# Hybrid Hyena and attention step: the weighted values of two query blocks in one PSUM bank of their own, and three banks for the seven-product pairs

## The chip, the cores and the metric

The kernel runs on one core of a Trainium2 chip. The metric is the device time of one execution in microseconds (us); lower is better. The core has a matrix engine (TensorE, "PE" in the profile; its weight loads are shown apart as "PEld"), a vector engine ("DVE"), a scalar engine ("ACT"), GpSimd ("POOL") and a queue that only issues transfers ("SP"). Products land in PSUM, which has eight banks of 128 partitions by 512 float32 values. Each engine works through its own instructions in the order in which they were put into its queue, and waits there for what an instruction needs.

## The reference, cut to what matters

One layer of a model with two parallel branches: a long convolution (Hyena) and attention. The change touches the attention branch. 512 latent queries attend to an 8 x 16 window of keys around them, plus 128 cached context keys, in one softmax; 128 prompt queries attend to the 128 prompt keys. There are 16 heads of 64 channels.

```python
s_win = einsum("brqhd,brkhd->bhrqk", qg, kg) * scale       # windowed keys, plus a learned bias
s_ctx = einsum("brqhd,bkhd->bhrqk", qg, ctx_k) * scale     # cached keys
p = softmax(concatenate([s_win, s_ctx], axis=-1), axis=-1)
o = einsum("bhrqk,brkhd->brqhd", p[..., :n_slab], vg) \
  + einsum("bhrqk,bkhd->brqhd", p[..., n_slab:], ctx_v)    # the weighted values
out = merge_branches(y_h, g_h, y_a, g_a, m, w_bh, w_ba, w_out)   # y_a * silu(g_a), projections, gates
x_new = layer_norm(ALPHA * x + gate * out, ln_g, ln_b)
```

## The kernel before, in words

The columns of every activation are the 640 tokens: 128 prompt tokens and 512 latent ones, the latter reordered into eight blocks of 64. Projections use each float32 operand as a high and a low part and add three products (high·high, high·low, low·high). A plain projection (line 177) fills two PSUM banks, one for each half of 320 columns.

Most projections of the attention stage are done two weight tiles at a time by `pair_tile` (lines 1167 to 1206): a 2 x 2 block product with seven products instead of eight. Each product is twelve matmuls of 128 x 320 into one of four PSUM tiles, x, y, v, z, in the order x, y, v, z, x, v, z; the last three add onto what is already there. Between the products the vector and scalar engines read the banks: after product 0 the scalar engine copies x to a tile `u` (line 1189); after product 1 the vector engine adds y to it (line 1191, "the u add"), which is the last read of y; after products 2, 3, 5 and 6 the vector engine adds v or z to that sum (line 1197); after product 4 the finished x is used directly. These four tiles come from `acc`, a pool of four banks that are handed out in turn; the other four banks, `aux`, serve all shorter uses.

There are 19 such pairs in the attention stage (queries and keys, attention gates, merge gates) and four more for `w_ba` afterwards. A generator `attend(j)` for each of the eight pairs of heads j is woven into them. It has *visits*, `tiled(i)` (lines 1084 to 1100), each for two query blocks of 128: the scores of the two blocks and two heads go into four `aux` banks; then come the weighted values of the two blocks of two visits earlier; then the softmax of the new scores. `turned(i)` transposes the probabilities of the last visit through `aux` banks and copies them to `pts` tiles. The weighted values of one block, `block_values` (lines 1071 to 1077), are three chunks of 128 keys times two heads: six float32 matmuls that each have 64 value channels as weights and move 128 query columns (line 1026). They are written to columns 384 to 511 of one of the score banks of the new visit, which the scores leave free. `gated` (lines 1062 to 1069) multiplies the result with the gate on the vector engine and sends it to DRAM (`ya_d`). An odd visit also has the prompt's weighted values.

Order: in the attention stage and in the stage after it TensorE runs in program order, as the weaving wrote it (`manual_schedule`). The vector, scalar and GpSimd instructions are ordered by a planner that simulates the program: of the instructions that are ready in its simulation it takes the one that stands first in the program. In the last stage (`out_tile`, line 1534) TensorE is left to the planner too.

After the attention stage, eight plain projections for `w_bh` (two banks each from `acc`) run, then the four `w_ba` pairs, then five output tiles, of which the first four take two `acc` banks each. Counted over the whole program, `acc` has been called 78 times when the attention stage starts.

Of the kernel before, what the change touches and what calls it, by code (L numbers as in the profile page):

```python
# [19 lines left out]
NT = 640  # L20
# [26 lines left out]
def tile_hyena_natten_step(ctx: ExitStack, tc: tile.TileContext, a, o):  # L47
# [59 lines left out]
    def split(dst_h, dst_l, src, eng=None):  # L107
        hi = nc.scalar.activation(dst_h, src, AF.Copy)  # L108
# [715 lines left out]
    def rows(h):  # L824
        return slice(64 * h, 64 * h + 64)
# [161 lines left out]
    def probs(j, b, s, tm):  # L987
# [15 lines left out]
        return res  # L1003

    CHUNKS = (
        ((2, 128), (1, 0), (None, 256)),
        ((2, 0), (3, 256), (None, 128)),
        ((3, 0), (4, 256), (None, 128)),
        ((4, 128), (1, 256), (None, 0)),
    )  # L1010

    def transposed(j, b, ps):
        res = []
        for h in range(2):
            pt = aux(f"pt{j}_{h}_{b}")
            parts = [ps[h][:, c : c + P] for _, c in CHUNKS[b]] + ([head[j]["pp"][:, h]] if b == 2 else [])
# [3 lines left out]
            ptS = at.tile([P, 384 if b % 2 else 512], F32, tag=f"pts{b % 2}", bufs=2, name=f"pts{j}_{h}_{b}")  # L1020
            nc.scalar.activation(ptS[:, :n], pt[:, :n], AF.Copy)
            res.append(ptS)
        return res

    def pvm(dst, lhs, rhs, start, stop):
        nc.tensor.matmul(dst, lhs, rhs, start=start, stop=stop, skip_group_check=True)  # L1026
# [33 lines left out]
        return out[f"v{j // 2}"][:, c : c + 64]  # L1060

    def gated(j, o_, *spans):
        yo = tp.tile([P, P], F32, tag="yo", bufs=3, name=f"yo{j}")
        c0 = 0
        for cols in spans:
            n = cols.stop - cols.start
            nc.vector.tensor_tensor(yo[:, c0 : c0 + n], out[f"sg{j}"][:, cols], o_[:, c0 : c0 + n], op=ALU.mult)
# [11 lines left out]
    def prompt_values(j, o_):  # L1079
        for h in range(2):  # L1080
            pvm(o_[rows(h)], val(j, 0, h), head[j]["t", 2][h][:, 384:], True, True)
        gated(j, o_, PS_)

    def tiled(i):
        ns = [n for n in (2 * i, 2 * i + 1) if n < 4 * NK]
        ss = {n: [aux(f"s{n}_{h}") for h in range(2)] for n in ns} or {0: [aux(f"ov{i}_{h}") for h in range(2)]}
        spare = [t[:, 384:] for n, pair in ss.items() if n % 4 or not ns for t in pair]
# [5 lines left out]
        j, b = divmod(2 * i - 4, 4)  # L1093
        if b == 2 and j >= 0:
            if not spare:
                spare.append(aux(f"op{j}")[:, 384:])
            prompt_values(j, spare.pop(0))
            del head[j]
# [26 lines left out]
    RING = ("wh", "wl", "wl", "wh", "wl")  # L1125

    ready, high, loads = {}, {}, {}

    def prepare(i0, i1, pin):
# [8 lines left out]
        s_cols = 512 if i0 >= T_BH else NT  # L1138

        def wsum(j, x, y, op, dst=None):  # L1140
            src[j] = dst if dst is not None else sp.tile([P, s_cols], F32, tag="s", bufs=3 if i0 >= T_BH else 2, name=f"s{j}_{i0}")[:, :512]
# [24 lines left out]

    def pair_tile(i0, i1, use, operand=operand):
        def halfrow(tag, bufs, name):
            return sp.tile([P, HALF if i0 >= T_BH else 384], F32, tag=tag, bufs=bufs, name=f"{name}{i0}")[:, :HALF]

        if i0 not in ready:
            prepare(i0, i1, False)
        wb, prep = ready.pop(i0)
        ps = {}
        for j in range(7):
            if j < 4:
                ps["xyvz"[j]] = acc(f"sp{i0}_{j}")[:, :HALF]
            dst, x = ps["xyvzxvz"[j]], operand(ORDER[j])
            for k in range(4):
                wh, wl = (wb[j][:, i, P * k : P * k + P] for i in range(2))  # L1180
                for i, (wk, xi) in enumerate(((wh, 0), (wh, 1), (wl, 0))):
                    nc.tensor.matmul(  # L1182
                        dst, wk, x(xi, k), start=j < 4 and k == 0 and i == 0, stop=k == 3 and i == 2, skip_group_check=True,
                    )
                if k == 1:
                    yield
            if j == 0:
                u = halfrow("u", 1, "u")
                nc.scalar.activation(u, dst, AF.Copy)
            elif j == 1:  # L1190
                nc.vector.tensor_tensor(u, dst, u, op=ALU.add)
            elif j == 4:
                use(0, 0, dst)
            else:
                if j != 3:
                    c = halfrow("c", 4, f"c{j}_")
                after = nc.vector.tensor_tensor(c, dst, c if j == 3 else u, op=ALU.add)  # L1197
# [25 lines left out]
    def mix(m):  # L1223
        t0, dst = (T_MH, mh_d) if m < 4 else (T_MA, ma_d)
        n0 = 2 * (m % 4)

        def use(i, hf, src):
            th = sp.tile([P, 384], F32, tag="c", bufs=4, name=f"th{m}")[:, :HALF] if hf == i == 0 else src
# [482 lines left out]
```

## Time and profile before

| what | value |
|---|---|
| time, median of 3 runs | 861.96 us (860.74 to 863.33) |
| profiled execution, span from first to last instruction | 859.1 us |
| time around the span, taken as median less span | 2.9 us |
| TensorE busy in the span | 849.4 us (99%) |
| VectorE busy | 678.7 us (79%) |
| ScalarE busy | 464.7 us (54%) |
| GpSimd busy | 131.4 us (15%) |
| mean granted TensorE clock | 0.998 |

The profile lists one execution. Only the span of that execution is in it; what lies around the span is taken as the difference to the median. A busy TensorE is not one at its best: matmuls overlap in a pipeline, and a group's mean is the duration of one from start to end, not the distance to the next. The distance between starts is what adds up; it is read from rows that give the start of a run of matmuls and their count.

### The profile page before, as it was taken

Reading aid. Unit: us, or ns where it says so; the run is one execution under the profiler, and the core shown is the slowest. Engines: PE = TensorE matmul, PEld = TensorE weight load, DVE = VectorE, ACT = ScalarE, POOL = GpSimd, SP = SyncE. Lnnn points to the kernel's source line nnn. Section 1 sums busy time; section 2 is a strip of 40 time slices with the busy share of each in tenths; the row PEclk is TensorE's granted clock in tenths of the full one; section 3 lists DMA queues with packets and bytes.
Section 4 is the critical chain, followed back from the end, with each engine's and each line's share of the span. In section 5 each row is a group of like instructions: output and inputs, shape, how many; then the busy total and the mean of one; then the engine's idle time right before and its main releaser. Section 6 shows DMA issues by size and latency. Waiting matters only on the chain.

```text
span 859.1 us, 16817 instructions
## 1 busy us (share of the span) xinstructions
PE 849.4 (99%) x6387; PEld 822.7 (96%) x6387; DVE 678.7 (79%) x1408; ACT 464.7 (54%) x996; POOL 131.4 (15%) x140
## 2 busy tenths in 40 slices
PE   9999999999999999999999999999999999999996
PEld 7999999999999999999999999999999999999885
DVE  6777695697759559789988897889888778799776
ACT  4675656545554643646665676666655654345310
POOL 0010010101001010105232225124222200000000
PEclk9999999999999999999999999999999999999999
DMA  9986575656657558774263535354354386445621
GB/s 352 359 256 144 109 149 126 153 122 144 127 134 150 126 146 187 168 251 148 85 195 90 192 95 189 106 177 149 105 173 118 111 266 202 173 131 140 246 107 54
DMA packets 56868, 138.64 MB, mean 161 GB/s; under 512 B 8495, under 2 KB 23859, under 8 KB 56788
## 3 DMA queue, kind: packets, MB, share of 16 engines
q1 hardware_dynamic: 45412, 111.69, 39.7%
q0 software_dynamic: 5760, 20.19, 14.4%
q10 hardware_dynamic: 5616, 5.70, 1.9%
q8 instruction: 50, 0.82, 0.4%
q14 instruction: 30, 0.25, 0.1%
HBM read 121.43 MB, written 16.12 MB: 160 GB/s over the span
## 4 chain that ended last, share of the span: by engine, by line
PE 95%; DMA 3%; DVE 1%; SPq 0%; ACT 0%; issue 0%; DVEq 0%
PE sp L1182 33%; PE mm L177 30%; PE out L1534 6%; PE v L917 5%; PE pt L1019 3%; PE s L1026 3%; PE s L979 2%; PE mm L191 2%; PE ve L929 1%; DMA raw<-wall 1%; DMA wl<-wall 1%; DMA ada<-wada 1%; PE adaT L262 1%; PE yb L166 1%; PE yb L165 1%; PE yb L167 1%
## 5 line engine op out<-in xcount | busy, mean ns | idle before, releaser
L1182 PE MATMUL sp<-t,wb 128*128 128x320 f32 x912 | 141.7, 310 | 0.0
L1182 PEld LDWEIGHTS sp<-t,wb 128*128 128x128 f32 x912 | 134.9, 188 | 0.9 <-ACT pp L1047 0.5
L1182 PE MATMUL sp<-hH,wb 128*128 128x320 f32 x456 | 111.2, 314 | 0.0
L177 PE MATMUL mm<-hH,wl 128*128 128x320 f32 x448 | 105.5, 309 | 0.1
L177 PE MATMUL mm<-hH,wh 128*128 128x320 f32 x448 | 104.9, 309 | 0.0
L177 PE MATMUL mm<-hL,wh 128*128 128x320 f32 x448 | 104.2, 310 | 0.0
L157 POOL DMA_DIRECT2D wl<-wall x37 | 32.2, 870 | 329.5 <-ACT wl L156 263.3
L108 ACT ACTIVATE wb<-s 128x512 fp32r<-128x512 f32 x92 | 56.3, 627 | 45.6 <-DVE s L1142 26.6
L1182 PEld LDWEIGHTS sp<-hH,wb 128*128 128x128 f32 x456 | 78.4, 188 | 2.3 <-issue 2.1
L158 ACT ACTIVATE wh<-raw 128x1024 fp32r<-128x1024 f32 x37 | 39.2, 1059 | 70.8 <-PE mm L177 65.3
L177 PEld LDWEIGHTS mm<-hH,wl 128*128 128x128 f32 x448 | 75.5, 188 | 0.9 <-DMA wl<-wall 0.4
L177 PEld LDWEIGHTS mm<-hH,wh 128*128 128x128 f32 x448 | 75.2, 188 | 0.5
L177 PEld LDWEIGHTS mm<-hL,wh 128*128 128x128 f32 x448 | 75.1, 188 | 0.3
L109 DVE TENSOR_TENSOR wb<-s,wb 128x512 fp32r<-128x512 f32 x92 | 62.5, 692 | 10.3 <-ACT wb L108 10.3
L1182 PE MATMUL sp<-hL,wb 128*128 128x320 f32 x228 | 70.4, 309 | 0.0
L108 ACT ACTIVATE wb<-raw 128x512 fp32r<-128x512 f32 x66 | 41.4, 628 | 44.4 <-PE sp L1182 23.5
L1001 POOL TENSOR_SCALAR p<-p,sm 128x384 f32<-128x384 f32 x32 | 44.5, 1399 | 102.7 <-DVE sm L1000 102.7
L109 DVE TENSOR_TENSOR wb<-raw,wb 128x512 fp32r<-128x512 f32 x66 | 46.6, 705 | 5.5 <-ACT wb L108 5.4
L177 PE MATMUL mm<-yhs,wh 128*128 128x320 f32 x256 | 47.9, 309 | 0.0
L1197 DVE TENSOR_TENSOR c<-sp,u 128x320 f32<-128x320 f32 x69 | 33.5, 486 | 12.0 <-PE sp L1182 12.0
L1182 PEld LDWEIGHTS sp<-hL,wb 128*128 128x128 f32 x228 | 42.8, 188 | 0.0
L1001 POOL TENSOR_SCALAR edge<-edge,sm 128x320 f32<-128x320 f32 x32 | 41.9, 1318 | 0.5 <-DVE sm L1000 0.5
(385 smaller groups left out, 2078.3 us busy)
## 6 DMA issues: line engine op xcount, KB each, us to landing
raw<-wall SPq DMA_DIRECT2D x93, 512.0 KB, 3.6
wl<-wall POOLq DMA_DIRECT2D x37, 512.0 KB, 5.8
ada<-wada SPq DMA_DIRECT2D x16, 512.0 KB, 9.2
tm<-bias SPq DMA_DIRECT2D x16, 512.0 KB, 4.5
xw<-xw SPq DMA_DIRECT2D x8, 512.0 KB, 9.4
gate<-wgate SPq DMA_DIRECT2D x8, 512.0 KB, 4.1
wo<-wall SPq DMA_DIRECT2D x8, 512.0 KB, 5.3
dec<-decay SPq DMA_DIRECT2D x20, 128.0 KB, 3.0
```

The source lines that it names most:

```text
L108: hi = nc.scalar.activation(dst_h, src, AF.Copy)
L109: return hi, (eng or nc.vector).tensor_tensor(dst_l, src, f(dst_h), op=ALU.subtract)
L157: nc.gpsimd.dma_start(wl, a["wall"][i], accum_op=ALU.add)
L158: nc.scalar.activation(wh, raw[:], AF.Copy)
L177: nc.tensor.matmul(ps[hf][:, :HALF], wt[k], x[:, hf * HALF : (hf + 1) * HALF], start=(i == 0 and k == 0), stop=(i == lead[2] and k == NK - ...
L917: nc.tensor.matmul(ps[t // 2][:, t % 2 * 256 : t % 2 * 256 + 256], x[:, k, P * t : P * t + P], wk, start=first and t % 2 == 0, stop=last, ...
L1001: nc.gpsimd.tensor_scalar_mul(pv, pv, sm[:, 2:3])
L1019: nc.tensor.transpose(pt[:, i * P : i * P + P], x, ident)
L1026: nc.tensor.matmul(dst, lhs, rhs, start=start, stop=stop, skip_group_check=True)
L1182: nc.tensor.matmul(dst, wk, x(xi, k), start=j < 4 and k == 0 and i == 0, stop=k == 3 and i == 2, skip_group_check=True,)
L1197: after = nc.vector.tensor_tensor(c, dst, c if j == 3 else u, op=ALU.add)
L1534: ins = nc.tensor.matmul(dst, m[k][:, c0 : c0 + P], w[:, c : c + n], start=(first and k == 0), stop=(last and k == 5), skip_group_check=True,)
```

## The change

Three things change.

1. The weighted values. `half_values` replaces `block_values` and `prompt_values`. It does a visit's two blocks together, in a bank of its own (`acc` number 3). Of the three key chunks of each of the two blocks, two are shared by both blocks (one chunk of window values, and the cached ones): these become one matmul of 256 columns, its moving operand two runs of 128 columns that lie 256 apart. The other chunk of each block stays a matmul of 128 columns. The probabilities' transposes are laid out so that this works: one `pts` tile of 896 columns for both blocks of a head, with the chunks in another order. The matmuls of a visit go from twelve to eight, their columns stay 1536. `gated` then runs once for 256 columns (even half), or for 192 + 64 and for the prompt's 128 (odd half): four vector operations and four transfers for each pair of heads, where there were six of each. Its buffer `yo` is 256 columns wide with two copies, before 128 with three.
2. The pairs of the attention stage. Bank 3 being taken, x, y, v, z get three banks: (0, 1, 2, 1) and (0, 2, 1, 2) in turn. z now has the bank of y of the same pair. The pairs after the attention stage keep four fixed banks (0, 1, 2, 3). `acc` calls without a number still go round all four; calls of pairs no longer move that count.
3. Widths of some scratch tiles (`c`, `u`, `s`) are cut to what is used, which makes room in SBUF.

```diff
-    ps_mm = ctx.enter_context(tc.tile_pool(name="ps_mm", bufs=4, space=PSUM))
+    ps_mm = ctx.enter_context(tc.tile_pool(name="ps_mm", bufs=1, space=PSUM))
-    def acc(name):
-        return ps_mm.tile([P, 512], F32, tag="mm", name=name)
+    turn_of = [0]
+    def acc(name, i=None):
+        if i is None:
+            i = turn_of[0] % 4
+            turn_of[0] += 1
+        return ps_mm.tile([P, 512], F32, tag=f"mm{i}", name=name)
...
+    PARTS = (
+        ((2, 128, None), (1, 0, 0), (3, 640, 1), (None, 256, None)),
+        ((4, 256, None), (3, 128, 0), (1, 768, 1), (None, 384, None)),
+    )
...
-    def block_values(n, o_):
-        j, b = divmod(n, 4)
-        for i, (t, _) in enumerate(CHUNKS[b]):
+    def half_values(j, half):
+        o_ = acc(f"o{j}_{half}", 3)
+        pts = head[j]["t", half]
+        for i, (t, c, b) in enumerate(PARTS[half]):
             for h in range(2):
                 lhs = head[j]["cv"][:, rows(h)] if t is None else val(j, t, h)
-                pvm(o_[rows(h)], lhs, head[j]["t", b][h][:, i * P : i * P + P], i == 0, i == 2)
-        gated(j, o_, *((slice(192 + P * b, 320 + P * b),) if b < 3 else (slice(576, NT), B7)))
+                if b is None:
+                    pvm(two(o_[rows(h), : 2 * P]), lhs, two(pts[h][:, c : c + 4 * P])[:, :, :P], i == 0, i == 3)
+                else:
+                    pvm(o_[rows(h), P * b : P * b + P], lhs, pts[h][:, c : c + P], False, False)
+        if half:
+            for h in range(2):
+                pvm(o_[rows(h), 2 * P : 3 * P], val(j, 0, h), pts[h][:, :P], True, True)
+            gated(j, o_, slice(448, NT), B7)
+            gated(j, o_[:, 2 * P :], PS_)
+            del head[j]
+        else:
+            gated(j, o_, slice(192, 448))
...
     def tiled(i):
...
-        for n in (2 * i - 4, 2 * i - 3):
-            if n >= 0:
-                block_values(n, spare.pop(0))
+        if i >= 2:
+            half_values(*divmod(i - 2, 2))
...
     def turned(i):
-        for n in (2 * i - 2, 2 * i - 1):
-            j, b = divmod(n, 4)
-            st_ = head[j]
-            st_["t", b] = transposed(j, b, st_[b])
+        j, half = divmod(i - 1, 2)
+        ptS = head[j]["t", half] = [at.tile([P, 896], F32, tag="pts", bufs=2, name=f"pts{j}_{half}_{h}") for h in range(2)]
+        for b in (2 * half, 2 * half + 1):
+            transposed(j, b, head[j][b], ptS)
...
+        pairs_done[0] += 1
+        home = (0, 1, 2, 3) if i0 >= T_BH else ((0, 1, 2, 1), (0, 2, 1, 2))[pairs_done[0] % 2]
         for j in range(7):
             if j < 4:
-                ps["xyvz"[j]] = acc(f"sp{i0}_{j}")[:, :HALF]
+                ps["xyvz"[j]] = acc(f"sp{i0}_{j}", home[j])[:, :HALF]
```

More of the change, by code (lines that the diff above doesn't have):

```diff
@@ L1005, in tile_hyena_natten_step, with transposed @@
     CHUNKS = (
-        ((2, 128), (1, 0), (None, 256)),
-        ((2, 0), (3, 256), (None, 128)),
+        ((1, 0), (2, 128), (None, 256)),
+        ((2, 0), (None, 128), (3, 256)),
         ((3, 0), (4, 256), (None, 128)),
-        ((4, 128), (1, 256), (None, 0)),
+        ((4, 128), (None, 0), (1, 256)),
     )
-    def transposed(j, b, ps):
-        res = []
+    PARTS = (
+        ((2, 128, None), (1, 0, 0), (3, 640, 1), (None, 256, None)),
+        ((4, 256, None), (3, 128, 0), (1, 768, 1), (None, 384, None)),
+    )
+    def transposed(j, b, ps, ptS):
         for h in range(2):
             pt = aux(f"pt{j}_{h}_{b}")
-            parts = [ps[h][:, c : c + P] for _, c in CHUNKS[b]] + ([head[j]["pp"][:, h]] if b == 2 else [])
+            parts = ([head[j]["pp"][:, h]] if b == 2 else []) + [ps[h][:, c : c + P] for _, c in CHUNKS[b]]
             n = P * len(parts)
@@ L1019, in transposed @@
                 nc.tensor.transpose(pt[:, i * P : i * P + P], x, ident)
[L1020 to L1023, printed above, removed]
+            c0 = (0, 384, 0, 512)[b]
+            nc.scalar.activation(ptS[h][:, c0 : c0 + n], pt[:, :n], AF.Copy)
     def pvm(dst, lhs, rhs, start, stop):
@@ L1062, in gated @@
     def gated(j, o_, *spans):
-        yo = tp.tile([P, P], F32, tag="yo", bufs=3, name=f"yo{j}")
+        yo = tp.tile([P, 2 * P], F32, tag="yo", bufs=2, name=f"yo{j}")
         c0 = 0
@@ L1069, in gated @@
             c0 += n
[L1071 to L1073 removed]
+    def half_values(j, half):
+        o_ = acc(f"o{j}_{half}", 3)
+        pts = head[j]["t", half]
+        for i, (t, c, b) in enumerate(PARTS[half]):
             for h in range(2):
                 lhs = head[j]["cv"][:, rows(h)] if t is None else val(j, t, h)
[L1076 to L1082 removed]
+                if b is None:
[10 more added lines that the diff above has]
+            gated(j, o_, slice(192, 448))
     def tiled(i):
         ns = [n for n in (2 * i, 2 * i + 1) if n < 4 * NK]
[L1086 to L1087 removed]
+        ss = {n: [aux(f"s{n}_{h}") for h in range(2)] for n in ns}
         for n in ns:
             block_scores(n, ss[n])
[L1090 to L1098 removed]
+        if i >= 2:
+            half_values(*divmod(i - 2, 2))
         for n in ns:
@@ L1127, in tile_hyena_natten_step @@
     ready, high, loads = {}, {}, {}
+    pairs_done = [0]
     def prepare(i0, i1, pin):
@@ L1137, in prepare @@
         wb = {}
-        s_cols = 512 if i0 >= T_BH else NT
         def wsum(j, x, y, op, dst=None):
-            src[j] = dst if dst is not None else sp.tile([P, s_cols], F32, tag="s", bufs=3 if i0 >= T_BH else 2, name=f"s{j}_{i0}")[:, :512]
+            src[j] = dst if dst is not None else sp.tile([P, 512], F32, tag="s", bufs=3 if i0 >= T_BH else 2, name=f"s{j}_{i0}")[:]
             ins = nc.vector.tensor_tensor(src[j], x, y, op=op)
@@ L1168, in halfrow @@
         def halfrow(tag, bufs, name):
-            return sp.tile([P, HALF if i0 >= T_BH else 384], F32, tag=tag, bufs=bufs, name=f"{name}{i0}")[:, :HALF]
+            return sp.tile([P, HALF], F32, tag=tag, bufs=bufs, name=f"{name}{i0}")[:]
         if i0 not in ready:
@@ L1227, in use @@
         def use(i, hf, src):
-            th = sp.tile([P, 384], F32, tag="c", bufs=4, name=f"th{m}")[:, :HALF] if hf == i == 0 else src
+            th = sp.tile([P, HALF], F32, tag="c", bufs=4, name=f"th{m}")[:] if hf == i == 0 else src
             nc.scalar.activation(th, src, AF.Tanh, scale=0.5)
```

## The prediction

> **What bounds the kernel now.** I read the page's first part, then busy time by stage, then the chain of waits.
>
> ```profile
> span 859.1 us, 16817 instructions
> PE 849.4 (99%) x6387; PEld 822.7 (96%) x6387; DVE 678.7 (79%) x1408; ACT 464.7 (54%) x996; POOL 131.4 (15%) x140
> ```
> ```profile
> 384.00:688.00 304.00, 304.00 (x2442) 294.35 (x2441) 259.03 (x671) 190.71 (x492) 95.31 (x80) 1.00 0.44 138
> ```
> ```profile
> 368.43 5.66 PE v L917 x48
> 512.77 5.43 PE L1182 MATMUL sp<-t,wb 128*128 128x320 f32 x36
> ```
>
> The second row is the attention stage; its columns after the window are the total, then busy time of PE, PEld, DVE, ACT and POOL, the granted clock and the DMA share. TensorE has work in flight in all of its 304 us, at full clock, while the vector engine is busy for 259. So nothing is gained there by making another engine faster or by shortening a wait that TensorE does not make: time falls only if TensorE's own instructions take less, and it rises by each new stop of TensorE. The last row, from the timeline, gives the price of a product: the last of 36 matmuls ends 5.43 us after the first starts and lasts 0.31, so starts are 5.12 / 35 = 0.146 us apart, and a product of twelve takes 1.76 us.
>
> **Part 1: the merged products.** Their price now, and rows for other widths:
>
> ```profile
> L1026 PE MATMUL s<-pts,v x252: 272/273/323, 413.9 to 665.5; 128*64 128x128 f32 x126
> ```
> ```profile
> 510.82 0.61 PE L1026 MATMUL s<-pts,v 128*64 128x128 f32 x8
> 511.25 0.39 PE L1026 MATMUL s<-pts,cv 128*64 128x128 f32 x4
> ```
> ```profile
> L228 PE MATMUL ps_f<-hf,pack x4: 429/481/533, 9.5 to 9.9; 64*128 64x320 f32 x4
> L917 PE MATMUL v<-wl,hH x128: 276/279/283, 299.6 to 380.9; 128*128 128x256 f32 x128
> ```
>
> The program has 126 matmuls of window and prompt values on score banks; the trace has 252 records, so a plain float32 matmul runs as two. Eight records, four matmuls, take 511.25 − 510.82 = 0.43 us: 0.109 us a matmul of 128 columns. A 256-column one of this type does not occur before. Two rows bound it. L228 is the same float32 type at 320 columns: at best 429 ns from start to end against 273 for 128 columns, 156 ns for 192 columns more, 0.81 ns a column. By that 128 more columns cost 104 ns and a 256-column matmul 0.213 us, 5 ns under two of 128. L917 moves 256 columns, but its operands are the high and low parts, which need one record each; 48 in 5.66 us is 0.118 us, hardly over the 128-column price. I take L228, because the float32 type and the two records are what half_values keeps. Sixteen halves have four merged products each, 64 in all: 64 x 5 ns = **−0.3 us**; by the L917 end it would be 64 x (218 − 118) ns = −6.4 us.
>
> The Trainium skill, "TensorE: Matmul & The Clock Gate", section "Back-to-back issue gap", gives about 81 ns for a sustained matmul of 128 columns and 131 ns for one of 512; by a straight line between them 256 columns are about 98 ns, an estimate from that page, so 64 merges would save 64 x (162 − 98) ns = 4.1 us. The trace agrees neither on the 128-column price (109 ns) nor on the slope for this type (0.81 ns a column against 0.13), and it decides.
>
> The sixteen vector operations and sixteen transfers that go away lie on engines that TensorE does not wait for, and count as nothing. So does the shorter hold on the score banks. What hides them is that TensorE has no wait in the stage; without that a gate operation of 128 columns would be worth some 0.2 us.
>
> ```profile
> 509.87 0.32 PE L979 MATMUL s<-kl,q 64*128 64x320 f32 x2
> ```
> ```profile
> 511.98 0.29 DVE L1067 TENSOR_TENSOR yo<-sg,s 128x128 f32<-128x128 f32 x1
> 512.18 0.56 DVE L994 CUSTOM_DVE_ANT_0 p<-s,tm 128x384 f32<-128x384 f32 x1
> ```
>
> In this visit the scores end at 510.2 us, and the rows show something else that goes away: where a score bank also holds weighted values, its softmax (L994) starts only after the values are done and the gate has read them. With a bank apart the softmax of odd visits can start up to 2 us earlier. That pays nothing by itself, but it matters to part 2. The regrouped transposes have the same count and columns. A values group now needs both blocks' copies at its start; at the end of the stage, where visits are closest, the last of them ends at 672.51 and the group starts at 674.25, so this costs nothing.
>
> ```profile
> 672.02 0.49 ACT L1021 ACTIVATE pts<-pt 128x384 f32<-128x384 f32 x1
> ```
> ```profile
> 674.25 0.66 PE L1026 MATMUL ov<-pts,v 128*64 128x128 f32 x8
> ```
>
> **Part 2: z waits for y's bank.** Product 3 (z) may now start only when the u add has read y, one product after y was finished, where before it had a free bank. Behind it in TensorE's queue stands everything. Where y of one pair takes the bank of v of the last, or v that of z, two products lie between (3.5 us). The tightest such read ends at 477.91, for a product that starts at 479.14, 1.2 us later; I put these at nothing.
>
> ```profile
> 477.44 0.47 DVE L1197 TENSOR_TENSOR c<-sp,u 128x320 f32<-128x320 f32 x1
> ```
> ```profile
> 479.14 2.79 PE L1182 MATMUL sp<-t,wb 128*128 128x320 f32 x18
> ```
>
> The u add is late where the woven visit puts softmax work ahead of it in the vector engine's order. The pairs for queries and keys of heads 4 and 6 have the same picture:
>
> ```profile
> 495.90 5.43 PE L1182 MATMUL sp<-t,wb 128*128 128x320 f32 x36
> 575.50 5.43 PE L1182 MATMUL sp<-t,wb 128*128 128x320 f32 x36
> ```
> ```profile
> 498.71 0.73 DVE L109 TENSOR_TENSOR wb<-raw,wb 128x512 fp32r<-128x512 f32 x1
> 499.36 0.15 DVE L1000 RECIPROCAL sm<-sm 128x1 f32<-128x1 f32 x1
> 499.44 0.47 DVE L1191 TENSOR_TENSOR u<-sp,u 128x320 f32<-128x320 f32 x1
> ...
> 579.02 0.47 DVE L1191 TENSOR_TENSOR u<-sp,u 128x320 f32<-128x320 f32 x1
> ```
> ```profile
> 515.68 0.49 DVE L1191 TENSOR_TENSOR u<-sp,u 128x320 f32<-128x320 f32 x1
> ```
>
> The 36 matmuls are products 1, 2 and 3, so z starts after 24 of them: 495.90 + 24 x 0.146 = 499.41, while the u add ends at 499.91. How long TensorE needs after such a read I take from a place where it waits for one already:
>
> ```profile
> 794.20 0.51 DVE L1197 TENSOR_TENSOR c<-sp,u 128x320 f32<-128x320 f32 x1
> ```
> ```profile
> 794.83 1.96 PE L1182 MATMUL sp<-ya_t,wb 128*128 128x320 f32 x12
> ```
>
> The read ends at 794.71 and the product starts at 794.83: 0.12 us. So the stop is 499.91 + 0.12 − 499.41 = 0.62 us; at 575.50 the same sum gives 579.49 + 0.12 − 579.01 = 0.60. In the pair that starts its product 1 at 512.77 (quoted at the top), z starts at 516.28 and the read ends at 516.17, so 0.01 us is missing; the other sixteen pairs, summed in the same way, have 0.06 to 2.4 us between read and z; the first and the last of the nineteen are these, with 389.36 − 389.23 = 0.13 and (18 matmuls on) 678.34 − 677.38 = 0.96 us:
>
> ```profile
> 385.86 5.43 PE L1182 MATMUL sp<-t,wb 128*128 128x320 f32 x36
> 675.71 3.78 PE L1182 MATMUL sp<-t,wb 128*128 128x320 f32 x24
> ```
> ```profile
> 388.75 0.48 DVE L1191 TENSOR_TENSOR u<-sp,u 128x320 f32<-128x320 f32 x1
> 676.89 0.49 DVE L1191 TENSOR_TENSOR u<-sp,u 128x320 f32<-128x320 f32 x1 [0.78 <-PE sp L1182]
> ```
>
> Stops of those sixteen are under 0.1 us. Together **+1.2 us**. This term is the least certain: the planner orders the vector engine anew. Its lower end is 0 (every u add early enough, as it is in twelve pairs by 0.7 us or more), its upper end that all seven pairs for queries and keys stop for some 0.6 us, 4.2 us.
>
> **Part 3: where the banks meet after the attention stage.** 78 calls of acc leave the turn at bank 2 (78 mod 4), and pairs no longer move it. The last pair is the nineteenth, so its z is in bank 2: the first plain projection, which starts right behind it, wants that bank at once. Before, it got the banks of x and y, read long ago.
>
> ```profile
> 688.90 0.75 PE L177 MATMUL mm<-yhs,wh 128*128 128x320 f32 x4
> 747.08 0.31 PE L1182 MATMUL sp<-ya_hH,wb 128*128 128x320 f32 x1
> ```
> ```profile
> 689.10 0.49 DVE L1197 TENSOR_TENSOR c<-sp,u 128x320 f32<-128x320 f32 x1 [1.27 <-PE sp L1182]
> 747.13 0.88 DVE L561 SCALAR_TENSOR_TENSOR mh<-mh,mm 128x320 f32<-128x320 f32 x2 [2.40 <-PE mm L177]
> ```
>
> It would start at 689.59 + 0.12 = 689.71 in place of 688.90: **+0.8 us**. Eight projections use sixteen banks, so the last has banks 0 and 1, and the first w_ba pair now starts in bank 0, fixed, where it had bank 2. The two gate reads take 0.88 us and follow each other by some 0.40 (0.88 less the 0.49 of one such read), so the first ends at 747.13 + 0.88 − 0.40 = 747.61; with 0.12 that is 747.73 in place of 747.08: **+0.7 us**. Both stops are in TensorE's written order, so nothing can fill them.
>
> At the end the first output tile moves from the banks of x and y to those of v and z of the last pair, which are read last. Its matmuls now fill two holes in that pair:
>
> ```profile
> 792.79 0.39 PE L1534 MATMUL out<-woh,yhs 128*128 128x512 f32 x1
> ...
> 796.62 0.39 PE L1534 MATMUL out<-woh,yhs 128*128 128x512 f32 x1
> ...
> 798.69 0.31 PE L1182 MATMUL sp<-ya_hH,wb 128*128 128x320 f32 x1
> ```
>
> The holes are 794.83 − 792.79 = 2.04 and 798.69 − 796.62 = 2.07 us. The planner may fill them as well with the second output tile, which gets the banks of x and y, and needs no data that the first does not; I take 0, with 4.1 us as the other end.
>
> **The sum.** −0.3 + 1.2 + 0.8 + 0.7 = +2.4 us on the profiled 859.1 us of span; with the 2.9 us around it that is the median of 862.0, so **864.4 us**. Its own range is 863 to 866.
>
> **Rivals.**
> Faster: 256 columns of float32 cost what L917 pays. Then part 1 is −6.4 us and the whole −6.4 + 2.7 = −3.7: 858.3 us. It takes over once a merged product costs less than 218 − 2700/64 = 176 ns. For it speaks only that L917 moves 256 columns in 118 ns; against it the 429 ns of L228 and the two records. Chance 0.08. The rule of the Trainium skill cited above would be a smaller form of it, 4.1 in place of 6.4 us.
> The new wait hardly bites: softmax work of odd visits moves ahead and the planner places the u adds earlier, so part 2 is 0 and the sum −0.3 + 1.5 = +1.2: 863.2 us. For it: the L1067 row ahead of L994. Against: in the even visits that stop, the vector engine works without a pause up to the u add (DVE in the row: 6.10 of 6.10 us), and it saves one gate operation there, some 0.1 us.
>
> ```profile
> 493.80:499.90 6.10, 6.10 (x56) 5.93 (x53) 6.10 (x24) 5.04 (x15) 1.95 (x3) 1.00 0.36 107
> ```
>
> Chance 0.22.
> The holes stay empty: the planner has nothing for them, +4.1 us on top, 868.5 us. For it: the first tile's banks are busy to the last. Against: the second tile's are free. Chance 0.10. With u adds late at most pairs (+3.0 on top, 867.4 us), another 0.08.
>
> **From cases to numbers.** The forecast has 0.50; 0.02 is left for something else that helps. 0.3% is 2.6 us, about what a measurement of this kernel can tell from no change, and the forecast lies just inside it: a little over half of its chance falls within, the rest beyond. Same: 0.27 + 0.20 = 0.47. Slower: 0.23 + 0.18 + 0.02 = 0.43. Faster: 0.10. The range runs from under the case in which the waits hardly bite, 861.0, to near the empty holes, 868.0.
>
> **What would show it.** Right: products of 256 columns in the values group lasting about 377 ns (273 + 104) and the group of a visit as long as now, twelve of 0.109 or 1.3 us; waits of TensorE on the vector engine's L1191, some 0.6 us each in two or three pairs; a gap of about 0.8 us ahead of the first w_bh projection and of 0.7 ahead of the first w_ba pair; output matmuls still between the last pair's products. Wrong: merged products near 280 ns and a values group of under 1.1 us; no idle time at z; a stage shorter than 304 us.

## The result, and the profile after

The changed kernel takes 864.91 us (median; 864.45 to 867.36), the kernel before 861.27 us (860.74 to 863.33) in the same comparison: ratio 1.0037, 95% interval 1.0021 to 1.0052. It is 3.6 us slower, a little over the 0.3% that can be told from no change. The forecast was 864.4 us, +2.4 us; its range, 861.0 to 868.0, holds the result. The ratio is worked out from all runs of a comparison, so it is not quite that of the two medians.

The profiled execution after took 867.36 us, 1.8 us more than its span. First the page's head, then the attention stage in the view of busy time by stage, with the columns as before the change (total, then PE, PEld, DVE, ACT, POOL, clock, DMA share, GB/s), then TensorE's own waits from the first pair to the last (us in total, times, longest).

```profile
span 865.6 us, 16507 instructions
PE 852.8 (99%) x6259; PEld 819.4 (95%) x6259; DVE 678.6 (78%) x1392; ACT 463.3 (54%) x996; POOL 133.9 (15%) x140
```
```profile
384.00:688.00 304.00, 302.86 (x2298) 287.62 (x2298) 258.01 (x652) 190.69 (x494) 97.65 (x80) 1.00 0.43 138
```
```profile
PE sp L1188 <- DVE sm L1005: 0.8, 2, 0.4
PE mm L182 <- DVE c L1203: 0.7, 1, 0.7
PE sp L1188 <- ACT wb L113: 0.5, 1, 0.5
PE sp L1188 <- DVE ql L862: 0.3, 1, 0.3
```

In this stretch TensorE waited for nothing before. Now it waits five times, 2.3 us in all, and two of the four rows lead astray: they name a reciprocal (`sm`) and a weight split (`wb`, a high or low part of a weight tile), where the experiments below find the u add and the gate's read of a bank.

A stop costs more than its idle time. Behind one, the first matmul takes longer and the next follows later. Therefore I compare where products start. Take the first matmul of each product of the 23 pairs, and of each plain projection between them, in both traces, subtract, and count from the first pair, since the time ahead of it differs from execution to execution. The delay of the changed kernel then grows in six steps and is flat between them:

| where | delay, us | forecast |
|---|---|---|
| second pair, ahead of x | 0.48 + 0.07 | none |
| pair of head 2, ahead of z | 0.09 + 0.06 | under 0.1 |
| pair of head 4, ahead of z | 0.59 + 0.07 | 0.62 |
| pair of head 6, ahead of z | 0.57 + 0.07 | 0.60 |
| first w_bh projection | 0.82 + 0.08 | 0.8 |
| first w_ba pair | 0.69 + 0.07 | 0.7 |

The second number of a step is what the matmul behind the stop adds. The delay is 3.61 us at the start of the last pair, 3.92 at its last product and 4.17 at the end of the span; the last 0.25 us come after the last operation of the compute engines and were not followed. Most visits lie between these steps, and nothing moves there.

The pair of head 4, from the timeline after (start, duration, engine, line, operation). The weighted values, the last product ahead of z and the u add:

```profile
496.52 1.09 PE L1032 MATMUL o<-pts,v 128*64 128x256 f32 x12
...
497.97 0.41 PE L1188 MATMUL sp<-hH,wb 128*128 128x320 f32 x1
...
498.96 3.67 PE L1188 MATMUL sp<-t,wb 128*128 128x320 f32 x24
503.05 1.71 PE L1188 MATMUL sp<-t,wb 128*128 128x320 f32 x10 [0.42 <-DVE sm L1005]
```
```profile
501.71 0.72 DVE L114 TENSOR_TENSOR wb<-raw,wb 128x512 fp32r<-128x512 f32 x1
502.36 0.15 DVE L1005 RECIPROCAL sm<-sm 128x1 f32<-128x1 f32 x1
502.44 0.47 DVE L1197 TENSOR_TENSOR u<-sp,u 128x320 f32<-128x320 f32 x1
```

The values of the visit take 497.97 − 496.52 = 1.45 us, before they took 1.46. The u add ends at 502.91 by its row (502.90 in the trace), and z starts 0.15 us later. At all six steps the first matmul starts 0.146 or 0.147 us after the vector engine ends its read of the bank's old content: `ql` at the second pair, the u add at the three stops at z, `c` and the gate's read at the other two. The instructions that two of the waits name end later than that, `sm` 0.08 us and `wb` 0.10 us before the start. Without the wait, z could have started at 498.96 + 24 x 0.146 = 502.46: the stop is 0.59 us, where 0.62 were forecast, by the same instruction in the same place.

### The profile page after: what moved, and what is told of

It reads as the page before. It is cut to its first block, busy times and chain, and to the rows that moved or that the text cites. A ratio compares the mean times of both kernels' runs of the same rounds, so it can differ in the third digit from the quotient of the medians.

```text
span 865.6 us, 16507 instructions
## 1 busy us (share of the span) xinstructions
PE 852.8 (99%) x6259; PEld 819.4 (95%) x6259; DVE 678.6 (78%) x1392; ACT 463.3 (54%) x996; POOL 133.9 (15%) x140
## 4 chain that ended last, share of the span: by engine, by line
PE 92%; DVE 4%; DMA 1%; issue 1%; ACT 1%; SPq 0%; DVEq 0%; ACTq 0%
PE mm L182 32%; PE sp L1188 29%; PE out L1540 6%; PE v L922 5%; PE pt L1027 3%; PE o L1032 3%; PE s L984 2%; PE mm L196 2%; PE ve L934 1%; PE adaT L267 1%; DVE wb L114 1%; DVE s L1146 1%; DMA wo<-wall 1%; DMA ada<-wada 1%; PE yb L171 1%
## 5 line engine op out<-in xcount | busy, mean ns | idle before, releaser
L1006 POOL TENSOR_SCALAR edge<-edge,sm 128x320 f32<-128x320 f32 x32 | 43.7, 1377 | 1.0 <-DVE sm L1005 1.0
L182 PEld LDWEIGHTS mm<-yhs,wh 128*128 128x128 f32 x256 | 40.3, 188 | 1.3 <-ACT wh L113 0.9
```

Source lines behind the costliest of these rows:

```text
L182: nc.tensor.matmul(ps[hf][:, :HALF], wt[k], x[:, hf * HALF : (hf + 1) * HALF], start=(i == 0 and k == 0), stop=(i == lead[2] and k == NK - ...
L1006: nc.gpsimd.tensor_scalar_mul(pv, pv, sm[:, 2:3])
```

## The experiments

In the table, "start" is when the first pair starts against the kernel before (in the profiled execution); the other columns are delays counted from there, at the start of the last pair and at the end of the span.

| run | time, us | ratio to before, 95% interval | start | last pair | end |
|---|---|---|---|---|---|
| changed kernel | 864.91 | 1.0037, 1.0021 to 1.0052 | +2.37 | 3.61 | 4.17 |
| turn | 863.59 | 1.0022, 1.0009 to 1.0034 | +0.46 | 1.94 | 2.26 |
| swap | 864.43 | 1.0030, 1.0020 to 1.0040 | +0.22 | 2.15 | 2.63 |
| first | 866.67 | 1.0057, 1.0039 to 1.0076 | +3.56 | 3.06 | 4.57 |
| unmerged | 867.32 | 1.0068, 1.0050 to 1.0085 | +0.02 | 4.61 | 4.91 |
| banks | 867.55 | 1.0050, 1.0032 to 1.0068 | +2.24 | 4.03 | 4.48 |
| heads | 865.50 | 1.0044, 1.0029 to 1.0059 | +0.82 | 4.01 | 4.90 |
| all | 861.89 | 1.0007, 0.9989 to 1.0025 | −0.32 | −0.07 | 0.48 |
| ts | 863.29 | 1.0012, 0.9996 to 1.0027 | +0.47 | 0.47 | 1.83 |
| best | 861.23 | 0.9997, 0.9984 to 1.0010 | −0.10 | −0.06 | 0.42 |
| nodma | 861.96 | 1.0007, 0.9992 to 1.0022 | +3.69 | −0.08 | 0.54 |

Where an edit leaves the code around a stop as it was, the stop repeats from trace to trace to 0.01 or 0.02 us. The start varies by 4 us, whatever the kernel, and the medians carry that: the median of before, 861.3, plus the delay at the end differs from them by up to 1.8 us. So they can't carry a verdict on half a microsecond, and the delays, each from one profiled execution, have to. Each comparison has its own runs of the kernel before (medians 861.3 to 861.6).

**turn: where the banks meet.**

```diff
+    turn_of[0] = 0
     firsts = [proj(T_BH + n, yhH, yhL) for n in range(2)]
```

> Only the count of the four-bank turn is set back to 0 ahead of the w_bh projections: the first has the banks of x and v of the last pair of the stage, the last has 2 and 3, the first output tile 0 and 1; all else is the changed kernel. Theory (the two stops come from where the banks meet): the gap of 0.9 us ahead of the first w_bh projection and that of 0.76 us ahead of the first w_ba pair go, 0.3 us in the last pair too; 1.7 to 2.0 us off the changed kernel, the attention stage unchanged. Rival (the vector engine is late there whatever the bank, or the time goes back behind it): the gaps shrink, and what follows moves by less than 0.5 us.

The time falls to a ratio of 1.0022; the two stops are gone and those of the stage stay as they were. TensorE's timeline at the first w_ba pair, after and then in this run, and the waits of this run:

```profile
752.00 0.46 PE L182 MATMUL mm<-yhs,wl 128*128 128x320 f32 x2
752.98 0.39 PE L1188 MATMUL sp<-ya_hH,wb 128*128 128x320 f32 x1 [0.52 <-ACT wb L113]
753.21 0.30 PE L1188 MATMUL sp<-ya_hL,wb 128*128 128x320 f32 x1
```
```profile
749.18 0.46 PE L182 MATMUL mm<-yhs,wl 128*128 128x320 f32 x2
749.47 0.31 PE L1188 MATMUL sp<-ya_hH,wb 128*128 128x320 f32 x1
749.62 0.31 PE L1188 MATMUL sp<-ya_hL,wb 128*128 128x320 f32 x1
```
```profile
PE sp L1188 <- DVE sm L1005: 0.8, 2, 0.4
PE sp L1188 <- DVE ql L862: 0.3, 1, 0.3
```

Nothing was done to the weights, yet the wait that was put down to the split (`wb`, line 113) is gone: it was the bank. The delay at the last pair falls by 3.61 − 1.94 = 1.67 us (0.90 + 0.76 are 1.66), at the end by 4.17 − 2.26 = 1.91. The rival falls. The 0.24 us between these two come ahead of product 5 of the last pair; they are also missing in unmerged below, which has the banks of the changed kernel there, so they are not shown to come from the banks. The rows also show the price of a restart: the matmul behind the stop starts 753.21 − 752.98 = 0.23 us after the first, without a stop 0.15. That is the 0.06 to 0.08 behind each of the six steps.

**swap: who frees y's bank.**

```diff
             if j == 0:
                 u = halfrow("u", 1, "u")
-                nc.scalar.activation(u, dst, AF.Copy)
             elif j == 1:
-                nc.vector.tensor_tensor(u, dst, u, op=ALU.add)
+                nc.scalar.activation(u, dst, AF.Copy)
+                nc.vector.tensor_tensor(u, ps["x"], u, op=ALU.add)
```

> Only the two steps that make the sum u change places: after product 1 the scalar engine copies y to u, which frees the bank that z wants, and the vector engine then adds x, which is not written again before product 4. Theory (z waits for the u add because it stands behind softmax work on the vector engine): the stops ahead of z in the pairs for queries and keys of heads 2, 4 and 6 (0.15, 0.66 and 0.64 us in the trace after) go, 1.4 us off the changed kernel; the other stops stay. Rival (the scalar engine is as late in these visits, having exponentials ahead of the copy): the stops stay near 0.6 us or move to other pairs, and the time is within 0.5 us of the changed kernel.

All three stops at z are gone. Around the same z, TensorE, the scalar engine and the vector engine in this run:

```profile
496.63 4.56 PE L1188 MATMUL sp<-t,wb 128*128 128x320 f32 x30
```
```profile
499.58 0.42 ACT L1196 ACTIVATE u<-sp 128x320 f32<-128x320 f32 x1
```
```profile
499.39 0.72 DVE L114 TENSOR_TENSOR wb<-raw,wb 128x512 fp32r<-128x512 f32 x1
500.04 0.21 DVE L1005 RECIPROCAL sm<-sm 128x1 f32<-128x1 f32 x2
500.17 0.47 DVE L1197 TENSOR_TENSOR u<-sp,u 128x320 f32<-128x320 f32 x1
```

Thirty matmuls run at the usual distance ((4.56 − 0.31) / 29 = 0.147), and z is the one that follows the 24th, at 500.15. The vector engine's u add ends at 500.64, half a microsecond past that as in the changed kernel, and nobody waits, because y was copied by 500.00. So z waited for the read of y and not for the reciprocal beside it, and the vector engine is late there because softmax work and a weight split stand ahead. The delay at the last pair is 3.61 − 2.15 = 1.46 us smaller (0.15 + 0.66 + 0.64 = 1.45). At the end it is 4.17 − 2.63 = 1.54 us. The medians differ by only 0.5 us, which the spread of the start leaves open.

**first: x behind x.**

```diff
-        home = (0, 1, 2, 3) if i0 >= T_BH else ((0, 1, 2, 1), (0, 2, 1, 2))[pairs_done[0] % 2]
+        n_ = pairs_done[0]
+        home = (0, 1, 2, 3) if i0 >= T_BH or n_ == 1 else (1, 0, 2, 3) if n_ == 2 else ((0, 1, 2, 1), (0, 2, 1, 2))[n_ % 2]
```

> Only the first two pairs of the stage, in which no weighted values are made yet, use all four banks: (0, 1, 2, 3), then (1, 0, 2, 3), so x of the second pair has the bank of y of the first in place of that of x. Theory (x of the second pair waited for the vector engine's read of x of the first, the ql tile): the 0.48 us ahead of the second pair and the 0.07 behind it go, 0.5 us off the changed kernel, nothing else moves. Rival (the second pair waits for its weights or its operand, or y with the late bank waits in x's place): the start of the second pair or of its product 1 stays 0.4 to 0.5 us later than in the kernel before.

The second pair starts at once: 0.00 us against the kernel before, where it had 0.48 + 0.07. In the changed kernel, the rows of this stop are the last read of the first pair's x, by `q_half` for `ql`, and the product behind it:

```profile
400.26 0.21 DVE L862 SCALAR_TENSOR_TENSOR ql<-sp,q 128x64 fp32r<-128x64 f32 x1
```
```profile
400.00 0.31 PE L1188 MATMUL sp<-hH,wb 128*128 128x320 f32 x1
400.61 0.39 PE L1188 MATMUL sp<-hH,wb 128*128 128x320 f32 x1 [0.30 <-DVE ql L862]
```

That this is all of it, the delay at the last pair shows: 3.61 − 3.06 = 0.55 us. The kernel is no faster in time, for two reasons at other places than the edit. The profiled execution starts 3.56 us late, and in the last pair TensorE stands still for 1.0 us, for a transfer:

```profile
PE sp L1189 <- DMA wb<-wall: 1.0, 1, 1.0
```

**unmerged and heads: what merging is worth.**

```diff
-                    pvm(two(o_[rows(h), : 2 * P]), lhs, two(pts[h][:, c : c + 4 * P])[:, :, :P], i == 0, i == 3)
+                    for e in range(2):
+                        pvm(o_[rows(h), P * e : P * e + P], lhs, pts[h][:, c + 2 * P * e : c + 2 * P * e + P], i == 0 and e == 0, i == 3 and e == 1)
```

> Only the merged products of the weighted values are taken apart: each matmul of 256 columns becomes two of 128 in the same bank, twelve for each visit as before the change; operands, banks and vector work stay those of the changed kernel. Theory (a float32 matmul of 256 columns costs what two of 128 cost): the values of a visit take 1.456 us in place of 1.451, 0.1 us more over 16 visits, no difference that can be measured. Rival (merging is what saves time, and other losses hide it): a visit's values take 1.7 us or more, and the kernel is 4 us slower.

A visit took 495.86 − 494.35 = 1.51 us, the delay grew by about 0.06 at each of the sixteen visits, and came to 4.61 us at the last pair. Neither side had that: too much for the theory, too little for the rival. In this edit both blocks of head 0 come first, then both of head 1; before the change the heads alternated. So the second form:

```diff
+            for e in range(2 if b is None else 1):
+                for h in range(2):
+                    lhs = head[j]["cv"][:, rows(h)] if t is None else val(j, t, h)
+                    d, s = (P * e, c + 2 * P * e) if b is None else (P * b, c)
+                    pvm(o_[rows(h), d : d + P], lhs, pts[h][:, s : s + P], i == 0 and e == 0, i == 3 and e == 1)
```

> Merged products taken apart as in the run before, but the two heads of a half in turn (head 0 and head 1 of one block, then of the other), as in the kernel before. In the run before, with both blocks of one head in a row, a visit took 1.511 us. Theory (matmuls of the two heads that follow each other run side by side, so it is the order that cost 0.06 us): a visit takes 1.456 to 1.461 us, as before the change, and the merge saves 0.01 us a visit. Rival (the bank of its own, or the larger operand tile, costs the 0.06): a visit stays at 1.51 us, and merging saves 0.06 us a visit, 1 us in all.

A visit in unmerged, then in heads:

```profile
494.35 1.10 PE L1032 MATMUL o<-pts,v 128*64 128x128 f32 x16
495.27 0.66 PE L1032 MATMUL o<-pts,cv 128*64 128x128 f32 x8
495.86 0.41 PE L1189 MATMUL sp<-hH,wb 128*128 128x320 f32 x1
```
```profile
494.98 1.09 PE L1032 MATMUL o<-pts,v 128*64 128x128 f32 x16
495.90 0.61 PE L1032 MATMUL o<-pts,cv 128*64 128x128 f32 x8
496.44 0.42 PE L1187 MATMUL sp<-hH,wb 128*128 128x320 f32 x1
```

With alternating heads it is 496.44 − 494.98 = 1.46 us, as before the change. So the order of the heads is worth 0.05 us a visit, and the merge 0.01. The latter isn't kept: behind the values the products start 0.01 us earlier than in the kernel before, and a few products on at the same time again. Across the visits between the pairs of heads 2 and 4 the delay stays at 0.70 us in the changed kernel, and in heads too. What paces TensorE over such a stretch wasn't tried.

**banks: the pairs' banks alone.** Here the kernel before gets the new homes and the new turn; its values stay on the score banks.

```diff
...
-                ps["xyvz"[j]] = acc(f"sp{i0}_{j}")[:, :HALF]
+                ps["xyvz"[j]] = acc(f"sp{i0}_{j}", home[j])[:, :HALF]
```

> The kernel before, with only the homes of the pairs taken over: (0, 1, 2, 1) and (0, 2, 1, 2) in the stage, fixed banks after it, the turn as in the changed kernel; the weighted values stay as before, on score banks, and bank 3 lies idle in the stage. Theory (all of the loss comes from the banks of the pairs, nothing from the values): the stops are those of the changed kernel, about 0.55 us ahead of the second pair, 0.15, 0.65 and 0.65 at z in the pairs of heads 2, 4 and 6, 0.9 and 0.76 where the stage ends and where w_ba begins; the products end about 4 us later than before, as in the changed kernel. Rival (gates on a bank apart, merged values or other transfers cost or save something of their own): the sum of the stops differs from the changed kernel's by over 1 us.

All six steps are there, of the same sizes or up to 0.07 us larger (0.55, 0.16, 0.71, 0.71, 0.91, 0.77), and two more: 0.12 and 0.10 us at z in the pairs that follow those of heads 4 and 6. Together 4.03 us, 0.4 more than the changed kernel, so within the theory's bound. The two small ones are where 0.01 us was missing by the prediction's rows. In the changed kernel there is no stop there, but heads has 0.15 and 0.17 us, and unmerged 0.12 twice. The planner's order makes the difference: in banks, heads and unmerged a weight split of 0.68 us (`wb<-raw,wb`) stands ahead of the u add on the vector engine, in the changed kernel behind it. Heads, then the changed kernel, in the pair that follows that of head 4:

```profile
517.31 0.68 DVE L114 TENSOR_TENSOR wb<-raw,wb 128x512 fp32r<-128x512 f32 x1
517.90 0.49 DVE L1196 TENSOR_TENSOR u<-sp,u 128x320 f32<-128x320 f32 x1
```
```profile
518.87 0.47 DVE L1197 TENSOR_TENSOR u<-sp,u 128x320 f32<-128x320 f32 x1
519.25 0.86 DVE L114 TENSOR_TENSOR wb<-raw,wb 128x512 fp32r<-128x512 f32 x1
```

Of the 0.40 us that heads has over the changed kernel at the last pair, 0.32 come from these two stops: from the order that the planner chose, and not from what a merged matmul costs.

**all, ts and best: the repairs together.** The run all has the edits of turn, swap and first in one; ts leaves that of first out.

> The three repairs together: turn set back to 0 ahead of the w_bh projections, u copied from y by the scalar engine, four banks for the first two pairs. Theory (the stops are all of the loss): no stop on a bank is left up to the last pair, whose products start 0.0 to 0.2 us later than before, counted from the first pair; in the last pair itself up to 0.9 us stay, as in the run with the copy of y alone, whose order of output matmuls there it shares. The time is 0 to 1 us over the kernel before. Rival (the stops only move): another wait of 0.5 us or more shows up in the stage.

> Turn set back and u copied from y, the first two pairs on three banks. Theory: the kernel with all three repairs plus the 0.55 us ahead of the second pair and nothing else. Rival (that stop is hidden further on): the same time as with all three, in products counted from the first pair.

In both, no stop on a bank is left up to the last pair but the 0.55 us in ts: −0.07 and 0.47 us at its start. From there to the end, all loses another 0.55 us and ts 1.36, since in ts the transfer into product 4's weights lands later. Its row in ts, from the timeline:

```profile
793.72 0.41 PE L1188 MATMUL sp<-ya_hH,wb 128*128 128x320 f32 x1 [1.06 <-DMA wb<-wall]
```

Stops ahead of that pair no longer differ between the two but for the 0.55 us, so the rival of ts falls. In both, the output matmuls stand otherwise in the last pair than in the kernel before (1, 6 and 13 of them around its last products, not 9 and 9). So best keeps the copy of y out of the w_ba pairs:

```diff
             if j == 0:
                 u = halfrow("u", 1, "u")
-                nc.scalar.activation(u, dst, AF.Copy)
+                if i0 >= T_BH:
+                    nc.scalar.activation(u, dst, AF.Copy)
+            elif j == 1 and i0 < T_BH:
+                nc.scalar.activation(u, dst, AF.Copy)
+                nc.vector.tensor_tensor(u, ps["x"], u, op=ALU.add)
             elif j == 1:
                 nc.vector.tensor_tensor(u, dst, u, op=ALU.add)
```

> The three repairs, with the copy of y only in the pairs of the stage; the four w_ba pairs make u as the kernel before does, so the output matmuls stand in the last pair as there. Theory: up to the last pair the products start within 0.1 us of the kernel before, counted from the first pair; in the last pair they differ only by when a transfer that adds into a weight tile lands; in time the same as the kernel before, ratio 0.999 to 1.001. Rival (merged values and fewer vector operations and transfers are worth more than the 0.01 us a visit seen so far): 1 us or more faster than before.

861.23 us, ratio 0.9997 (0.9984 to 1.0010): the changed kernel without its stops is the kernel before, to 0.06 us at the last pair. At the end it is 0.42, in all 0.48, so the place of the output matmuls didn't matter. One wait of TensorE is left from the first pair on:

```profile
PE sp L1189 <- DMA wb<-wall: 0.2, 1, 0.2
```

So merged values, and fewer vector operations and transfers, bring nothing that can be measured, and the rival falls.

**nodma: the stop in the last pair.**

```diff
-            if i0 > T_BA and j in (4,):
+            if T_BA < i0 < T_BA + 6 and j in (4,):
```

> The run best, and in the last pair the low part of product 4's weights is made by the vector engine (0.68 us an operation) and not by a transfer that adds the weights in DRAM onto the high part. Theory (the stop of 0.2 to 1.1 us inside product 4 of the last pair, seen in the runs banks, heads, first, swap, all and ts, comes from that transfer, which took 5.7 to 7.2 us): it is gone, and the time is 0 to 0.5 us under best. Rival (the vector engine has no room there): products 5 or 6 of the last pair start 0.3 us or more later, and nothing is won.

The wait for the transfer is gone, but in the last pair product 5 has 0.53 us and product 6 0.60 more delay than product 4, and the end 0.54 in place of 0.42: the rival. The vector engine's last read of product 5's bank (`c<-sp,u`) ends at 798.91, 0.06 us before that product starts at 798.97; in best it ends at 794.64, and the product starts at 795.16. Counted from the start of the pair (787.61 and 783.83), the read ends 0.49 us later in nodma, which fits the added operation. That TensorE waits for this read is not shown: the profile names nothing, and 0.06 us is not the 0.15 of the other stops.

## Why the prediction was right or wrong

- *What bounds the kernel* was right: TensorE is the bound, each new stop shows in the end, and the work that went from the vector engine and the queues moved nothing. The run all, with the six stops taken out, is at −0.07 us.
- *Part 1, −0.3 us*: the mechanism was right, the size small and still too large. A merged product lasts 379 ns, 377 were forecast, and its group took 1.451 in place of 1.461 us; over a few products the 0.01 us is lost again, so the term is 0.0. The row of line 917 did not hold for this type, and the faster rival with it (the Trainium skill's rule, "TensorE: Matmul & The Clock Gate", section "Back-to-back issue gap", from which 4.1 us were estimated, finds no support in the runs: a visit takes 1.46 us in heads and 1.45 in the changed kernel, and best is no faster than before). The row:

```profile
L1032 PE MATMUL o<-pts,cv x64: 379/379/379, 417.7 to 690.0; 128*64 128x256 f32 x64
```

- *Part 2, +1.2 us*: the mechanism was right, and 1.45 us were measured. The u adds were as late as read off the trace of before: 0.59 and 0.57 for 0.62 and 0.60. Mis-sized is the restart, 0.07 a stop, which the sum didn't have, and the pair of head 2, 0.15 in place of under 0.1. The rival in which the wait hardly bites falls: the planner did not place the u adds earlier in the even visits. In the two pairs for which 0.01 us was missing it did place them earlier, which nothing in the prediction foresaw. The 0.12 us between a read and its product was misread: up to the product that it was taken from, TensorE in the kernel before has no idle time. Six output matmuls start 0.226 us apart from 793.47 on, the last at 794.60, and the product follows at the same distance:

```profile
793.47 1.52 PE L1534 MATMUL out<-wo,yhs 128*128 128x512 f32 x6
```

  That 0.12 came so near the 0.15 us of the six steps was luck.
- *Part 3, +0.8 and +0.7*: right, 0.90 and 0.76, the difference again the restart.
- *The holes of the last pair, 0*: they were filled, by the second output tile in place of the first, as the text held possible. 0.31 us came in that pair all the same: 0.24 ahead of product 5 and 0.07 behind its first matmul. Turn, where the first output tile has its banks back, has the 0.07 alone, but so has unmerged, where it has not. In the changed kernel's trace the vector engine waits 0.22 us for the scalar engine at 794.88, and product 5 starts 0.06 us after the vector engine's read of v ends; that would fit, and no run takes that wait away.
- *The step that failed* is in part 2: "Where y of one pair takes the bank of v of the last, or v that of z, two products lie between (3.5 us)", and then "I put these at nothing". x was left out of that list. With three banks x has bank 0 in every pair, so it waits for the x of the pair before, whose last read comes after product 4. In all pairs but one that read is in time; in the first pair it is the vector engine's `ql`, and that costs 0.55 us. The run first shows it. The picture of the kernel before was too simple there: "handed out in turn" is only roughly so, since its pool gives out the bank that came free first. By the built program's list of banks, x of a pair had the bank of y of the pair before, whose last read comes after product 1; by strict turns it would have had that of x, and the stop of 0.55 us with it. (By the same list the first w_ba pair had bank 1 before and not 2, which changes no number.)
- *The sum*: 0.0 + 1.45 + 0.90 + 0.76 + 0.55 = 3.66 us, measured 3.61 up to the last pair and 4.17 at the end of the span; forecast 2.4. That the time came out at 864.9 against 864.4 owes something to chance: the forecast started from a median of 862.0, of which the comparison gave 861.27; and about 1.8 us lie around a span, not the 2.9 that were taken as median less span, so the profiled execution of before was one of about 861 us.

## What to carry to other kernels

When accumulators lose a bank, list for each of them who reads the bank's former content last, which engine does it, and how many products lie between; the list has to have every accumulator in it, also the one whose bank looks unchanged. Then look for that read in the trace: where TensorE has no slack, a stop here was the end of the vector engine's read plus 0.15 us less the due start, and another 0.07 for the restart. Have a bank's early release done by the engine that has the time, and set a rotation of banks that is kept by a counter anew where calls leave it.

## What the runs showed of the hardware

**The beginning varies by 4 us.** The same group of 32 matmuls in the first microseconds, before the change and in the runs first and nodma:

```profile
10.28 1.42 PE L262 MATMUL adaT<-ada,st 128*32 128x128 f32 x32
```
```profile
13.03 1.94 PE L267 MATMUL adaT<-ada,st 128*32 128x128 f32 x32
```
```profile
12.79 1.94 PE L267 MATMUL adaT<-ada,st 128*32 128x128 f32 x32
```

Nothing in this part differs between the kernels, and no wait of that size stands there; the matmuls themselves take longer up to some 16 us, after which all runs go alike. In the profile after, the granted clock is recorded as 0.74 (5 to 10 us) and 0.58 (10 to 15 us), in first and nodma as 1.00, though the matmuls were slow there as well. The kernel before has the same spread (860.5 to 866.2 us over all comparisons). The Trainium skill, "TensorE: Matmul & The Clock Gate", section "What's actually happening", says that the throttle of the clock is released after a window of activity that runs free of the kernel's start, so that the slow beginning varies from run to run. The varying start agrees with that; the recorded clock doesn't in two of three profiles, and why it lasts to some 16 us is not shown.

**Two heads side by side.** Matmuls with 64 value channels as weights, one head beside the other, cost 0.05 us a visit more when a head's two blocks follow each other than when the heads alternate (1.51 and 1.46 us). That they run at the same time in the two halves of the array is the reading that fits; the Trainium skill has it for tiles of the array, "TensorE: Matmul & The Clock Gate", section "Part 3: Packing small matmuls — row/col tiling", and here only the order shows it.

**A transfer at the edge.** The one that adds weights in DRAM onto the tile for product 4 of the last pair takes 5.6 to 5.8 us in the profiles of before, after, turn and unmerged, where TensorE doesn't wait for it, and 6.4 to 7.5 in first, swap, banks, heads, all, ts and best, where it waits 0.2 to 1.1 us. First the row of the transfers between 780 and 800 us in the kernel before, then in ts (the last number is us from issue to landing):

```profile
wb<-wall POOLq DMA_DIRECT2D x1, 256.0 KB, 5.7
```
```profile
wb<-wall POOLq DMA_DIRECT2D x1, 256.0 KB, 7.5
```

None of the edits divides the two groups (unmerged is in time, heads late). With one profile of each kernel, it is not shown whether the late landing belongs to a kernel or to an execution.
